# A hybrid decoder block on one Trainium2 core: queries and keys transposed in fp32 and split on the way out of the PSUM bank, key blocks in a ring of three, rotary and softmax steps done for all heads at once

## The chip, the core and the metric

The kernel runs on one core of one Trainium2 chip. The core has five engines with a queue each: TensorE (PE, with its weight loads PEld), VectorE (DVE), ScalarE (ACT), GpSimd (POOL) and SyncE (SP, which here only issues transfers). The metric is the device time of one execution in microseconds (us), and lower is better.

## What is computed

The block takes x of 2048 tokens by 1024 channels through a layer norm, one input projection, windowed attention beside a gated unit, an output projection and a dense feed-forward part. The change lies in the attention:

```python
    q, k, v, su, sv = jnp.split(proj, splits, axis=-1)
    q = apply_partial_rope(q.reshape(b, s, N_Q_HEADS, HEAD_DIM), cos, sin)   # 8 heads of 64, 16 rotated
    k = apply_partial_rope(k.reshape(b, s, N_KV_HEADS, HEAD_DIM), cos, sin)  # 2 heads
    attn = sliding_window_attention(q, k, v, attn_sinks[l])
    ...
    # in sliding_window_attention, blocks of 128 tokens:
    kb, vb = band(k), band(v)                       # the block before and the current one
    scores = jnp.einsum('bnqkgd,bnskd->bnkgqs', qb, kb) * (HEAD_DIM ** -0.5)
    scores = jnp.where(allowed, scores, -1e30)      # each query sees 128 keys
    probs = jax.nn.softmax(jnp.concatenate([scores, sink], axis=-1), axis=-1)[..., :-1]
    out = jnp.einsum('bnkgqs,bnskd->bnqkgd', probs, vb)
```

All products that must be exact to fp32 are made from two reduced-precision parts of each operand, a high part (a rounded copy) and a low part (the value less its high part). "Split" means the making of the two.

## The kernel before

The tokens go through the first stage in 16 tiles of 128. For tile i the functions are, in words: `x_transpose` turns the normalised tile and splits it into `hT` (8 transposes into bank `pst`, an ACT copy for the high part, a DVE subtraction, L159, for the low part); `inproj` makes the key/value projection `pkv` (24 matmuls of 256 columns) and the query projection `pq` (24 of 512); `kv_post` and `q_post` add the bias, rotate 16 of every 64 channels (`rope`), and split the result in SBUF into `ks` and `qs` (L340/341 and L359/360); `k_transpose` turns the four 128-column pieces of `ks`, copies them to `kT` (L370), and copies the block once more (L373) into the next tile's `kT`, so that each tile has its own pair of blocks; `q_transpose` turns the eight pieces of `qs` (L380) and copies them out (L382); `scores` makes 16 matmuls in two groups of four heads (banks `ps_0`, `ps_1`), selects the 128 keys that are seen (`copy_predicated`), takes the maximum, and runs eight exponentials per tile on ACT; `softmax` divides on POOL (L425); `p_transpose` turns the probabilities (`pt`), splits them (`hl`) and masks them on POOL (L443); `pv` multiplies them by v (`po`), and the result is stored.

The main loop (L642) runs tile i's scores beside the projections of tile i+2 and the transposes of tile i+3. POOL's order in this stage is the order of the program (`manual_schedule`). On the other engines a scheduler sets the order when the program is built; each engine then works through its own list strictly in order. The buffers limit it: `ps2` has 2 PSUM buffers of 1024 columns, which `pst`, `ps_0`, `ps_1` and the query transposes take in turn, and `ps1` has 4 of 512 columns, taken in turn by the rest. `ps_1` of a tile lands in the buffer from which `hT` was read just before. POOL does, per tile, two products of the softmax, `x*g_in` (L680), four masks (L443), `x+b_in` (L692) and a small power.

After the 16 tiles come the gated unit (matmuls `psv`, `pu`, `pm`), the output projection (`pw`) and the feed-forward part, which takes from about 710 us to the end. They are not touched.

## Time and profile before

| | |
|---|---|
| median of 3 runs (lowest, highest) | 2070.11 us (2068.48, 2766.5) |
| the profiled execution's own time | 2070.19 us |
| its span, first to last instruction | 2068.5 us |
| mean granted TensorE clock | 0.981 |
| busy: PE, DVE, ACT, POOL | 95%, 70%, 37%, 21% of the span |
| PE, DVE, POOL busy between 100 and 300 us (200 us) | 181.0, 179.5, 133.2 us |
| PE busy between 1000 and 1500 us (500 us) | 499.8 us |

Busy times are sums over an engine's instructions. Over the whole span PE is the bound. In the first 350 us, where the change lies, DVE is as busy as PE. [...]

### The profile page before, as it was taken

Reading aid. Unit: us, or ns where it says so; the run is one execution under the profiler, and the core shown is the slowest. Engines: PE = TensorE matmul, PEld = TensorE weight load, DVE = VectorE, ACT = ScalarE, POOL = GpSimd, SP = SyncE. Lnnn points to the kernel's source line nnn. Section 1 sums busy time; section 2 is a strip of 40 time slices with the busy share of each in tenths; the row PEclk is TensorE's granted clock in tenths of the full one; section 3 lists DMA queues with packets and bytes.
Section 4 is the critical chain, followed back from the end, with each engine's and each line's share of the span. In section 5 each row is a group of like instructions: output and inputs, shape, how many; then the busy total and the mean of one; then the engine's idle time right before and its main releaser. Section 6 shows DMA issues by size and latency. Waiting matters only on the chain.

```text
span 2068.5 us, 25063 instructions
## 1 busy us (share of the span) xinstructions
PE 1967.7 (95%) x9326; PEld 1621.9 (78%) x9326; DVE 1453.0 (70%) x2497; ACT 762.1 (37%) x1484; POOL 443.2 (21%) x378
## 2 busy tenths in 40 slices
...
GB/s 197 97 107 102 108 138 178 239 102 102 182 199 199 105 171 69 84 90 65 90 82 71 120 135 72 92 79 74 92 57 96 229 208 219 188 165 190 160 117 102
DMA packets 137010, 267.60 MB, mean 129 GB/s; under 512 B 8244, under 2 KB 79924, under 8 KB 133304
## 3 DMA queue, kind: packets, MB, share of 16 engines
...
q8 instruction: 73, 1.20, 0.2%
...
## 4 chain that ended last, share of the span: by engine, by line
issue 38%; PE 37%; DVE 14%; DMA 6%; ACT 2%; POOL 2%; SPq 0%; POOLq 0%; ACTq 0%; DVEq 0%
PE X_d L943 10%; PE Z_d L943 5%; PE pu L575 4%; PE psv L537 4%; PE X_g L943 3%; PE Y_d L943 3%; DMA acc<-in_x 2%; DMA h2d<-acc 2%; PE pq L314 2%; PE Z_g L943 1%; PE pw L809 1%; PE pkv L314 1%; POOL aD L993 1%; DVE st L124 1%; DVE acc L798 1%
## 5 line engine op out<-in xcount | busy, mean ns | idle before, releaser
L844 ACT ACTIVATE ws<-s 128x512 fp32r<-128x512 f32 x176 | 109.9, 627 | 303.4 <-PE Z_g L943 152.7
L993 POOL DMA_DIRECT2D aD<-x x44 | 23.5, 534 | 858.4 <-DVE x L991 839.0
L809 PE MATMUL pw<-wo,m 128*128 128x512 f32 x768 | 178.3, 391 | 0.0
L809 PEld LDWEIGHTS pw<-wo,m 128*128 128x128 f32 x768 | 143.0, 188 | 29.1
L845 DVE TENSOR_TENSOR ws<-s,ws 128x512 fp32r<-128x512 f32 x176 | 121.1, 690 | 58.5 <-ACT ws L844 57.1
L943 PE MATMUL Z_g<-t1t_h,ws 128*128 128x512 f32 x528 | 138.0, 398 | 0.5 <-DVE ws L845 0.5
L943 PE MATMUL Y_g<-b21t_h,wa 128*128 128x512 f32 x528 | 137.2, 394 | 0.0
L943 PE MATMUL X_g<-t2t_h,ws 128*128 128x512 f32 x528 | 130.9, 396 | 3.0 <-ACT x L973 3.0
L943 PE MATMUL X_g<-b11t_h,wa 128*128 128x512 f32 x528 | 132.6, 398 | 0.3 <-ACT wa L844 0.3
L943 PE MATMUL Z_g<-b22t_h,ws 128*128 128x512 f32 x528 | 130.4, 395 | 1.7 <-ACT ws L844 1.7
L943 PE MATMUL X_g<-t3t_h,ws 128*128 128x512 f32 x528 | 130.5, 395 | 0.2 <-ACT x L973 0.2
L943 PE MATMUL X_g<-t4t_h,wa 128*128 128x512 f32 x528 | 130.1, 395 | 0.0
L844 ACT ACTIVATE ws_d<-s_d 128x512 fp32r<-128x512 f32 (+1 forms) x96 | 55.7, 593 | 188.8 <-PE X_d L943 51.1
L845 DVE TENSOR_TENSOR wa<-rw,wa 128x512 fp32r<-128x512 f32 x132 | 90.2, 686 | 47.7 <-ACT wa L844 47.5
L943 PEld LDWEIGHTS X_g<-t2t_h,ws 128*128 128x128 f32 x528 | 99.6, 189 | 27.1 <-ACT x L973 3.4
L943 PEld LDWEIGHTS Z_g<-t1t_h,ws 128*128 128x128 f32 x528 | 100.0, 190 | 25.0 <-DVE ws L845 1.0
L943 PEld LDWEIGHTS X_g<-b11t_h,wa 128*128 128x128 f32 x528 | 100.3, 190 | 24.4 <-ACT wa L844 0.7
L943 PEld LDWEIGHTS Z_g<-b22t_h,ws 128*128 128x128 f32 x528 | 99.3, 188 | 25.7 <-ACT ws L844 2.2
L943 PEld LDWEIGHTS X_g<-t3t_h,ws 128*128 128x128 f32 x528 | 99.2, 188 | 24.2 <-ACT x L973 0.7
L943 PEld LDWEIGHTS Y_g<-b21t_h,wa 128*128 128x128 f32 x528 | 99.2, 188 | 23.8 <-ACT wa L844 0.2
L943 PEld LDWEIGHTS X_g<-t4t_h,wa 128*128 128x128 f32 x528 | 99.3, 188 | 23.5
L991 DVE TENSOR_TENSOR x<-X_g,x 128x512 f32<-128x512 f32 x44 | 30.4, 690 | 115.7 <-PE X_g L943 115.7
...
## 6 DMA issues: line engine op xcount, KB each, us to landing
...
hTg<-hTd POOLq DMA_DIRECT2D x16, 1024.0 KB, 10.4
...
```

The lines of the kernel that those rows point to most:

```text
L124: V.bn_stats(st[:, j, :], src[:, j * 512:(j + 1) * 512])
L314: PE.matmul(ps[:, :c1_ - c0], t[:, a, k, :], wq[k][:, b, c0:c1_], start=(k == 0 and n == 0), stop=(k == KT - 1 and n == 2))
L537: PE.matmul(pv_, t[:, a, k, :], wsv_t[k][:, b, :], start=(k == 0 and n == 0), stop=(k == KT - 1 and n == 2))
L575: PE.matmul(pu[:, j, :], wsu_t[k][:, a, hs], t[:, b, k, :], start=(k == 0 and n == 0), stop=(k == KT - 1 and n == 2))
L798: V.tensor_tensor(ac, ac, ag, ALU.mult)
L809: PE.matmul(po[:, c * 512:(c + 1) * 512], m[k // 4][:, a, kc], wo[k][c][:, b, :], start=(k == 0 and n == 0), stop=(k == KT - 1 and n == 2))
L844: A.activation(hi, src, AF.Copy)
L845: V.tensor_tensor(lo, src, f32b(hi), ALU.subtract)
L943: PE.matmul(bank[x_], lt[:, a, k, :], rt[:, b, k, :], start=(first and k == 0 and m == 0), stop=(k == nk - 1 and m == 2), skip_group_check ...
L991: V.tensor_tensor(v["x1"], ps, v["x1"], ALU.mult)
L993: PL.dma_start(aD[g][h][:, e, :], v["o"].rearrange("p a t -> p (a t)"))
```

## The change

- **Queries and keys.** They are no longer split in SBUF. `kv_post` writes each key head twice and the values into one fp32 tile `qkv` (tag `qs`, now two buffers), `q_post` adds the queries. PE turns that tile: two transposes for the keys instead of four, four for the queries instead of eight. The split happens out of PSUM: ACT copies the high part, DVE subtracts for the low part (L355 and L369 of the new file). For queries this is done in two halves of 64 partitions.
- **Key ring.** `kT` is one tile with three blocks; the copy of a block for the next tile goes.
- **Rotary.** One pass of three DVE instructions over 12 heads (8 query heads and 4 key copies) takes the place of two passes of four.
- **Scale.** The factor 1/8 moves from the query's bias step into the exponential.
- **Softmax.** The shift `nm`, the sink term `es`, the sum and the reciprocal are made once for 8 heads instead of twice for 4; both groups' maxima come first, and then all eight exponentials.
- **Banks.** The query transposes take a `ps1` buffer and no longer a `ps2` buffer. Loads and tiles that borrowed the old tags borrow other ones.

```diff
     def qbias():
         V.tensor_scalar(nsink, sink, -1.0, None, ALU.mult)
 
-        V.tensor_scalar(bqkv[:, :ATTN], bqkv[:, :ATTN], SCALE, None, ALU.mult)
...
-    kTt = {}
+
+    kT = c1.tile([P, NKV, 2, 3, P], F32R, name="kT")
     vd = {}
     qTt = {}
-
-    def new_kT(i):
-        kTt[i] = wk.tile([P, NKV, 2, 2, P], F32R, tag="kT", name=f"kT{i}")
-
-    new_kT(0)
...
-    def rope(i, t, nh, nm):
-        rot = t.rearrange("p (h d) -> p h d", d=HD)[:, :, :ROT]
-        rot = rot.rearrange("p h (a b) -> p h a b", a=2)
-        t1 = wk.tile([P, nh, 2, HALF], F32, tag="rt1" + nm, bufs=1, name=f"rt1{nm}_{i}")
-        t2 = wk.tile([P, nh, 2, HALF], F32, tag="rt2" + nm, bufs=1, name=f"rt2{nm}_{i}")
-        cb = cos2[:, i].unsqueeze(1).broadcast_to([P, nh, 2, HALF])
-        V.tensor_tensor(t1, rot, cb, ALU.mult)
-        for a in range(2):
-            sb = sin2[:, i, a].unsqueeze(1).broadcast_to([P, nh, HALF])
-            V.tensor_tensor(t2[:, :, a], rot[:, :, 1 - a], sb, ALU.mult)
-        V.tensor_tensor(rot, t1, t2, ALU.add)
+
+    NR = NQ + 2 * NKV
 
     def kv_post(i):
         ps = pproj.pop((i, "kv"))
-        kv = wk.tile([P, QKV - ATTN], F32, tag="kv", bufs=1, name=f"kv{i}")
-        V.tensor_tensor(kv, ps[:, :QKV - ATTN], bqkv[:, ATTN:], ALU.add)
-        rope(i, kv[:, :P], NKV, "k")
-        ks = wk.tile([P, NKV, 2, 2, HD], F32R, tag="ks", bufs=1, name=f"ks{i}")
-        kb = kv[:, :P].rearrange("p (g d) -> p g d", g=NKV).unsqueeze(2)
-        kb = kb.broadcast_to([P, NKV, 2, HD])
-        A.activation(ks[:, :, 0], kb, AF.Copy)
-        V.tensor_tensor(ks[:, :, 1], kb, f32b(ks[:, :, 0]), ALU.subtract)
-        qks[i, "k"] = ks
-        qks[i, "v"] = kv
+        t = wk.tile([P, NR * HD + P], F32, tag="qs", name=f"qkv{i}")
+        kk = [v_.rearrange("p (g d) -> p g d", g=NKV).unsqueeze(2).broadcast_to([P, NKV, 2, HD])
+              for v_ in (ps[:, :P], bqkv[:, ATTN:ATTN + P])]
+        V.tensor_tensor(t[:, ATTN:NR * HD].rearrange("p (g e d) -> p g e d", g=NKV, e=2), *kk,
+                        ALU.add)
+        V.tensor_tensor(t[:, NR * HD:], ps[:, P:2 * P], bqkv[:, ATTN + P:], ALU.add)
+        qks[i] = t
 
     def v_post(i):
-        kv = qks.pop((i, "v"))
-        v3 = kv[:, P:].rearrange("p (g d) -> p g d", g=NKV)
+        v3 = qks[i][:, NR * HD:].rearrange("p (g d) -> p g d", g=NKV)
         vd[i] = wk.tile([P, NKV, 2, HD], F32R, tag="vd", bufs=4, name=f"vd{i}")
         A.activation(vd[i][:, :, 0], v3, AF.Copy)
         V.tensor_tensor(vd[i][:, :, 1], v3, f32b(vd[i][:, :, 0]), ALU.subtract)
 
     def q_post(i):
         ps = pproj.pop((i, "q"))
-        q = wk.tile([P, ATTN], F32, tag="q", bufs=1, name=f"q{i}")
-        V.scalar_tensor_tensor(q, ps, SCALE, bqkv[:, :ATTN], ALU.mult, ALU.add)
-        rope(i, q, NQ, "q")
-        q3 = q.rearrange("p (h d) -> p h d", d=HD)
-        qs = wk.tile([P, NQ, 2, HD], F32R, tag="qs", bufs=1, name=f"qs{i}")
-        V.tensor_copy(qs[:, :, 0, :], q3)
-        V.tensor_tensor(qs[:, :, 1, :], q3, f32b(qs[:, :, 0, :]), ALU.subtract)
-        qks[i, "q"] = qs
+        t = qks[i]
+        V.tensor_tensor(t[:, :ATTN], ps, bqkv[:, :ATTN], ALU.add)
+        rot = t[:, :NR * HD].rearrange("p (h d) -> p h d", d=HD)[:, :, :ROT]
+        rot = rot.rearrange("p h (a b) -> p h a b", a=2)
+        t1 = wk.tile([P, NR, 2, HALF], F32, tag="rt1q", bufs=1, name=f"rt1_{i}")
+        t2 = wk.tile([P, NR, 2, HALF], F32, tag="rt2q", bufs=1, name=f"rt2_{i}")
+        cb = cos2[:, i].unsqueeze(1).broadcast_to([P, NR, 2, HALF])
+        sb = sin2[:, i].unsqueeze(1).broadcast_to([P, NR, 2, HALF])
+        V.tensor_tensor(t1, rot, cb, ALU.mult)
+        V.tensor_tensor(t2, rot[:, :, ::-1, :], sb, ALU.mult)
+        V.tensor_tensor(rot, t1, t2, ALU.add)
 
     def k_transpose(i):
-        ks = qks.pop((i, "k"))
-        pk = ps1.tile([P, 512], F32, tag="one", name=f"pk{i}")
-        kf = f32b(ks.rearrange("p g a b d -> p (g a b d)"))
-        for j in range(4):
-            PE.transpose(pk[:, j * P:(j + 1) * P], kf[:, j * P:(j + 1) * P], ident)
-        pk4 = pk.rearrange("p (g a t) -> p g a t", g=NKV, a=2)
-        A.activation(kTt[i][:, :, :, 1, :], pk4, AF.Copy)
-        if i + 1 < NT:
-            new_kT(i + 1)
-            V.tensor_copy(kTt[i + 1][:, :, :, 0, :], f32b(kTt[i][:, :, :, 1, :]))
+        pk = ps1.tile([P, 512], F32, tag="one", name=f"pk{i}")[:, :NKV * P]
+        for g in range(NKV):
+            c = (NQ + 2 * g) * HD
+            PE.transpose(pk[:, g * P:(g + 1) * P], qks[i][:, c:c + P], ident)
+        pk = pk.rearrange("p (g t) -> p g t", g=NKV)
+        r = i % 3
+        A.activation(kT[:, :, 0, r, :], pk, AF.Copy)
+        V.tensor_tensor(kT[:, :, 1, r, :], pk, f32b(kT[:, :, 0, r, :]), ALU.subtract)
 
     def q_transpose(i):
-        qs = qks.pop((i, "q"))
-        pq = ps2.tile([P, D], F32, tag="two", name=f"pq{i}")
-        qf = f32b(qs.rearrange("p h a d -> p (h a d)"))
-        for j in range(NQ):
-            PE.transpose(pq[:, j * P:(j + 1) * P], qf[:, j * P:(j + 1) * P], ident)
-        qT = wk.tile([P, NQ, P], F32R, tag="qT", bufs=1, name=f"qT{i}")
-        A.activation(qT.rearrange("p h t -> p (h t)"), pq, AF.Copy)
+
+
+        pq = ps1.tile([P, 512], F32, tag="one", name=f"pq{i}")
+        for j in range(NQ // 2):
+            PE.transpose(pq[:, j * P:(j + 1) * P], qks[i][:, j * P:(j + 1) * P], ident)
+        qks.pop(i)
+        qT = wk.tile([P, 2, NQ // 2, P], F32R, tag="qT", bufs=1, name=f"qT{i}")
+        for e in range(2):
+            own, other = slice(e * HD, (e + 1) * HD), slice((1 - e) * HD, (2 - e) * HD)
+            hi = qT[own, e].rearrange("p h t -> p (h t)")
+            A.activation(hi, pq[own], AF.Copy)
+            V.tensor_tensor(qT[other, e].rearrange("p h t -> p (h t)"), pq[own], f32b(hi),
+                            ALU.subtract)
         qTt[i] = qT
 
     pr = {}
 
     def scores(i):
         qT = qTt.pop(i)
-        kT = kTt.pop(i)
-        c0 = 1 if i == 0 else 0
+        r = i % 3
+        blocks = slice(r, r + 1) if i == 0 else (slice(0, 3, 2) if r == 0 else slice(r - 1, r + 1))
+        cur = 1 if r or i == 0 else 0
         mx = wk.tile([P, NQ], F32, tag="mx", name=f"mx{i}")
         nm = wk.tile([P, NQ], F32, tag="nm", name=f"nm{i}")
         sm = wk.tile([P, NQ], F32, tag="sm", name=f"sm{i}")
         es = wk.tile([P, NQ], F32, tag="es", name=f"es{i}")
+        pbs = []
         for g in range(NKV):
-            ps = ps2.tile([P, G, 2 * P], F32, tag="two", name=f"ps{i}_{g}")
+            ps = ps2.tile([P, G, 2, P], F32, tag="two", name=f"ps{i}_{g}")
             pb = wk.tile([P, G, P], F32, tag="pb", bufs=3, name=f"pb{i}_{g}")
             for j in range(G):
                 for a in range(2):
-                    PE.matmul(ps[:, j, c0 * P:], qT[:, g * G + j, :],
-                              kT[:, g, a, c0:].rearrange("p c t -> p (c t)"),
-                              start=(a == 0), stop=(a == 1))
+                    PE.matmul(ps[:, j, 1:] if i == 0 else ps[:, j], qT[:, j % 2, (g * G + j) // 2, :],
+                              kT[:, g, a, blocks], start=(a == 0), stop=(a == 1))
             if i == 0:
                 PL.memset(pb, NEG)
             else:
-                A.activation(pb, ps[:, :, :P], AF.Copy)
-            V.copy_predicated(pb, curb, ps[:, :, P:])
+                A.activation(pb, ps[:, :, 1 - cur], AF.Copy)
+            V.copy_predicated(pb, curb, ps[:, :, cur])
             gs = slice(g * G, (g + 1) * G)
             V.tensor_reduce(mx[:, gs], pb, op=ALU.max, axis=mybir.AxisListType.X)
-            V.scalar_tensor_tensor(nm[:, gs], mx[:, gs], -1.0, nsink[:, gs], ALU.mult, ALU.min)
-            V.tensor_tensor(es[:, gs], sink[:, gs], nm[:, gs], ALU.add)
-            for j in range(G):
-                h = g * G + j
-                A.activation(pb[:, j, :], pb[:, j, :], AF.Exp, bias=nm[:, h:h + 1],
-                             accum_out=sm[:, h:h + 1])
-            A.activation(es[:, gs], es[:, gs], AF.Exp)
-            pr[i, g] = (pb, sm, es)
+            pbs.append(pb)
+        V.scalar_tensor_tensor(nm, mx, -SCALE, nsink, ALU.mult, ALU.min)
+        V.tensor_tensor(es, sink, nm, ALU.add)
+        for h in range(NQ):
+            pb = pbs[h // G][:, h % G, :]
+            A.activation(pb, pb, AF.Exp, bias=nm[:, h:h + 1], scale=SCALE,
+                         accum_out=sm[:, h:h + 1])
+        A.activation(es, es, AF.Exp)
+        pr[i] = (pbs, sm, es)
 
     def softmax(i):
-        for g in range(NKV):
-            pb, sm, es = pr[i, g]
+        pbs, sm, es = pr[i]
+        V.tensor_tensor(sm, sm, es, ALU.add)
+        V.reciprocal(sm, sm)
+        for g, pb in enumerate(pbs):
             gs = slice(g * G, (g + 1) * G)
-            V.tensor_tensor(sm[:, gs], sm[:, gs], es[:, gs], ALU.add)
-            V.reciprocal(sm[:, gs], sm[:, gs])
             PL.tensor_tensor(pb, pb, sm[:, gs].unsqueeze(2).broadcast_to([P, G, P]), ALU.mult)
 
...
-            tag, bufs = (("rq", 2), ("rq", 2), ("kT", 2), ("qs", 1))[j]
+            tag, bufs = (("rq", 2), ("rq", 2), ("qs", 2), ("qs", 2))[j]
...
-            gv = wk.tile([P, SGW], F32, tag="ks" if e else "q", bufs=1, name=f"gv{i}")
+            gv = wk.tile([P, SGW], F32, tag="qT" if e else "gv", bufs=1, name=f"gv{i}")
```

What the scheduler does with it on two engines, in the tile whose scores are number 9 (of 0 to 15). First TensorE, before: the piece from the transposes of tile 12 (`pst`) over the scores of tile 9 (`ps_0`, `ps_1`), the turning of tile 8's probabilities (`pt`) and tile 7's products with v (`po`) to the first matmuls of the next key projection (`pkv`).

```order
L156 MATMUL pst_2452<-ident,x_1870 128x128 x8
L400 MATMUL ps_0_2531<-kT_2174,qT_2396 128x256 x7
L434 MATMUL pt_0_2466<-ident,pb_0_2315 128x128 x4
L400 MATMUL ps_0_2531<-kT_2174,qT_2396 128x256
L434 MATMUL pt_1_2477<-ident,pb_1_2335 128x128 x4
L461 MATMUL po_0_2489<-pT_0_2263,vd_1650 128x512 x2
L461 MATMUL po_0_2489<-pT_0_2263,vd_1867 128x512 x2
L461 MATMUL po_1_2497<-pT_1_2274,vd_1650 128x512 x2
L461 MATMUL po_1_2497<-pT_1_2274,vd_1867 128x512 x2
L400 MATMUL ps_1_2551<-kT_2174,qT_2396 128x256 x8
L314 MATMUL pkv_2571<-wq_237,hT_2451 128x256 x3
```

`pst` stands right behind the query projection and ahead of the scores, and `ps_1`, which lands in the buffer of `pst`, comes 2 us of PE work later. The same piece of the changed kernel:

```order
L390 MATMUL ps_0_2302<-kT,qT_2179 128x256 x2
L390 MATMUL ps_1_2315<-kT,qT_2179 128x256 x2
L390 MATMUL ps_0_2302<-kT,qT_2179 128x256 x6
L390 MATMUL ps_1_2315<-kT,qT_2179 128x256 x6
L423 MATMUL pt_0_2237<-ident,pb_0_2108 128x128 x4
L423 MATMUL pt_1_2248<-ident,pb_1_2121 128x128 x4
L450 MATMUL po_0_2260<-pT_0_2056,vd_1509 128x512 x2
L450 MATMUL po_0_2260<-pT_0_2056,vd_1704 128x512 x2
L450 MATMUL po_1_2268<-pT_1_2067,vd_1509 128x512 x2
L450 MATMUL po_1_2268<-pT_1_2067,vd_1704 128x512 x2
L156 MATMUL pst_2418<-ident,x_1902 128x128 x8
L308 MATMUL pkv_2339<-wq_237,hT_2222 128x256 x3
```

`pst` has moved behind the scores and `po`: `ps_1` no longer follows it, and a whole tile of work lies between `pst` and the next use of its buffer. Over all tiles 0 to 13 the last `pst` transposes stand between the query projection and the scores in 13 before and in 5 now. Both groups' scores now stand together, the first two of each group ahead of the other six. The four query transposes stand behind `pkv` and the key transposes, ahead of the next query projection.

Then VectorE for the same tile, before, from the first selection (`pb_0`) to the first shift (`nm`) of tile 9:

```order
L407 COPY_PREDICATED pb_0_2532<-curm,ps_0_2531 128x512
L124 BN_STATS st<-x_2726 128x6 x2
L437 TENSOR_TENSOR hl_1_2482<-pt_1_2477,hl_1_2482 128x512
L466 TENSOR_TENSOR at_2488<-po_0_2489,plo_0_2494 64x512
L350 TENSOR_TENSOR vd_2506<-kv_2398,vd_2506 128x2x64
L466 TENSOR_TENSOR at_2488<-po_1_2497,plo_1_2502 64x512
L409 TENSOR_REDUCE mx_2527<-pb_0_2532 128x4
L407 COPY_PREDICATED pb_1_2552<-curm,ps_1_2551 128x512
L125 BN_AGGR mv<-st 128x2
L335 TENSOR_TENSOR kv_2615<-pkv_2571,bqkv 128x256
L410 SCALAR_TENSOR_TENSOR nm_2528<-mx_2527,nsink 128x4
```

and now:

```order
L396 COPY_PREDICATED pb_0_2303<-curm,ps_0_2302 128x512
L398 TENSOR_REDUCE mx_2298<-pb_0_2303 128x4
L426 TENSOR_TENSOR hl_0_2242<-pt_0_2237,hl_0_2242 128x512
L396 COPY_PREDICATED pb_1_2316<-curm,ps_1_2315 128x512
L426 TENSOR_TENSOR hl_1_2253<-pt_1_2248,hl_1_2253 128x512
L455 TENSOR_TENSOR at_2259<-po_0_2260,plo_0_2265 64x512
L331 TENSOR_TENSOR vd_2277<-qkv_2184,vd_2277 128x2x64
L398 TENSOR_REDUCE mx_2298<-pb_1_2316 128x4
L455 TENSOR_TENSOR at_2259<-po_1_2268,plo_1_2273 64x512
L159 TENSOR_TENSOR hT_2417<-pst_2418,hT_2417 128x1024
L400 SCALAR_TENSOR_TENSOR nm_2299<-mx_2298,nsink 128x8
```

The first shift stood behind one maximum; the second stood five rows further. Now the one shift stands behind both maxima and behind the subtraction for `hT`, and all eight exponentials wait for it. Behind it, in the same list, the sum `sm` waits for the exponentials, and the second half of the query split and the query's bias step stand behind `sm`.

## Rows read from the trace of the kernel before

**Rows 1.** Eleven tile periods: stretch, length, busy of PE, PEld, DVE, ACT, POOL, clock, DMA.

```profile
191.10:213.27 22.17, 16.80 (x97) 14.53 (x95) 20.33 (x43) 12.44 (x37) 15.91 (x13) 0.92 0.32 120
213.27:228.64 15.37, 15.37 (x103) 13.85 (x102) 13.03 (x31) 9.22 (x26) 10.13 (x9) 1.00 0.27 102
...
sum 195.87, PE 176.88 PEld 154.71 DVE 177.36 ACT 118.81 POOL 132.12; mean PE 16.08 PEld 14.06 DVE 16.12 ACT 10.80 POOL 12.01
```

**Rows 2.** Groups by line, PE, 99.85 to 295.72: busy, mean ns, idle before.

```profile
L400 PE MATMUL ps<-kT,qT 128*128 128x256 f32 x176 | 28.9, 306 | 12.1 <-DVE hT L159 10.4 <-ACT qT L382 1.7
...
L434 PE MATMUL pt<-ident,pb 128*128 128x128 f32 x88 | 13.7, 284 | 5.4 <-POOL pb L425 5.4
```

**Rows 3.** Timeline of PE: start, length, what, idle before and its releaser.

```profile
206.56 1.22 PE L400 MATMUL ps<-kT,qT 128*128 128x256 f32 x8 [3.82 <-DVE hT L159]
```

**Rows 4.** Timeline of DVE ahead of that wait.

```profile
201.42 2.76 DVE L360 TENSOR_TENSOR qs<-q,qs 128x512 fp32r<-128x512 f32 x1
...
205.30 1.20 DVE L159 TENSOR_TENSOR hT<-pst,hT 128x1024 fp32r<-128x1024 f32 x1
```

**Rows 5.** Timeline of POOL, the same and the next tile.

```profile
201.08 2.55 POOL L680 TENSOR_TENSOR x<-x,g_in 128x1024 f32<-128x1024 f32 x1 [0.90 <-ACT x L139]
...
217.43 1.08 POOL L425 TENSOR_TENSOR pb<-pb,sm 128x512 f32<-128x512 f32 x1 [0.37 <-DVE sm L424]
```

**Rows 6.** Groups by line, DVE, 99.85 to 295.72.

```profile
L360 DVE TENSOR_TENSOR qs<-q,qs 128x512 fp32r<-128x512 f32 x11 | 16.7, 1519 | 0.1
...
L410 DVE SCALAR_TENSOR_TENSOR nm<-mx,nsink 128x4 f32<-128x4 f32 x21 | 11.3, 538 | 0.0
L411 DVE TENSOR_TENSOR es<-sink,nm 128x4 f32<-128x4 f32 x22 | 10.7, 486 | 0.0
...
L329 DVE TENSOR_TENSOR rt2q<-q,sin 128x64 f32<-128x64 f32 x22 | 8.3, 413 | 0.0
L326 DVE TENSOR_TENSOR rt1q<-q,cos 128x128 f32<-128x128 f32 x11 | 8.1, 736 | 0.3
...
L373 DVE CAST kT<-kT 128x512 fp32r<-128x512 f32 x11 | 7.0, 639 | 0.5 <-ACT kT L370 0.5
...
L326 DVE TENSOR_TENSOR rt1k<-kv,cos 128x32 f32<-128x32 f32 x11 | 5.3, 485 | 0.0
L359 DVE CAST qs<-q 128x512 fp32r<-128x512 f32 x11 | 5.3, 485 | 0.4
...
L329 DVE TENSOR_TENSOR rt2k<-kv,sin 128x16 f32<-128x16 f32 x22 | 4.2, 217 | 0.0
...
L330 DVE TENSOR_TENSOR q<-rt1q,rt2q 128x128 f32<-128x128 f32 x11 | 3.2, 291 | 0.3
```

**Rows 7.** Timeline of PE in an unbroken tile period.

```profile
220.67 0.60 PE L434 MATMUL pt<-ident,pb 128*128 128x128 f32 x4
...
224.46 3.12 PE L314 MATMUL pkv<-wq,hT 128*128 128x256 f32 x24
227.41 1.04 PE L380 MATMUL pq<-ident,qs 128*128 128x128 f32 x8
228.28 0.60 PE L368 MATMUL pk<-ident,ks 128*128 128x128 f32 x4
228.64 0.71 PE L314 MATMUL pq<-wq,hT 128*128 128x512 f32 x2
```

**Rows 8.** Two DVE subtractions by line: count, shortest/median/longest ns.

```profile
L360 DVE TENSOR_TENSOR qs<-q,qs x16: 676/684/2758, 47.6 to 312.3; 128x512 fp32r<-128x512 f32 x16
...
L437 DVE TENSOR_TENSOR hl<-pt,hl x32: 625/674/691, 76.7 to 341.1; 128x512 fp32r<-128x512 f32 x32
```

**Rows 9.** Timelines at the start: PE, then DVE.

```profile
55.93 0.90 PE L368 MATMUL pk<-ident,ks 128*128 128x128 f32 x3 [2.58 <-DVE ks L341]
...
19.38 1.75 DVE L288 TENSOR_SCALAR bqkv<-bqkv 128x512 f32<-128x512 f32 x1
```

**Rows 10.** The last weight loads (`rsu`) into borrowed buffers, from issue to landing.

```profile
DMA to landing us min/median/max: 4.9/4.9/4.9
```

5 lines of the change are left out of this document (2 added, 3 removed).

## The prediction

> **What bounds the kernel now.** I looked first at the busy shares by slices of time: after 710 us TensorE is busy nearly without a break, and the change touches nothing there. The loop that it touches was then cut into tile periods, each from the start of one tile's query projection to the start of the next. Eleven of them fill 195.87 us, so a tile takes 17.81 us. TensorE is busy for 16.08 us of it and VectorE for 16.12 [rows 1]: neither is the bound by itself, and each loses time to the other. One period shows what TensorE needs when nothing holds it: 15.37 us, all 103 matmuls recorded, no idle time, clock 1.00. [...] So a mean tile loses 17.81 - 15.37 = 2.44 us: 195.87 - 176.88 = 18.99 us of waiting over eleven tiles, 1.73 each, and 16.08 - 15.37 = 0.71 of matmuls that run slower, mostly in periods that had waits.
>
> The groups by line say whom TensorE waits for: the scores for VectorE's subtraction that makes `hT`, 10.4 us in eleven tiles (0.95 a tile), and the turning of the probabilities for POOL's product, 5.4 us (0.49) [rows 2]. One case in the timelines: at 206.56 the scores start after a wait of 3.82 us for `hT` [rows 3]. VectorE made that `hT` at 205.30, late because its subtraction for the query split (L360) took 2.76 us [rows 4]. The usual length of that one is 0.684 [rows 8]. Beside it POOL ran `x*g_in` from 201.08 for 2.55 us, to 203.63 [rows 5], and the subtraction ended at 204.18, just behind. I read this as VectorE held while POOL works on SBUF. L437, a subtraction of the same shape that reads a PSUM bank, is 625 to 691 ns in all 32 cases; L360, which reads SBUF alone, goes from 676 to 2758 [rows 8].
>
> **The change, part by part.** The profiled execution took 2070.19 us, the median is 2070.11, so the sum may be set against either. Tiles 0 to 13 go through this loop, fourteen periods.
>
> *TensorE.* Eight query transposes take 228.28 - 227.41 = 0.87 us of its queue, 0.109 each, and four key transposes 0.36, 0.09 each [rows 7]. Four and two fall away: 0.435 + 0.18 = 0.62 us a tile. The unbroken period goes from 15.37 to 14.75. Score and projection matmuls keep shape and number; the ring's strided blocks and the other bank I cost at nothing, as weights and columns are as many as before.
>
> *VectorE* [rows 6]. The rotary of the queries is 0.736 + 2 x 0.413 + 0.291 = 1.85 us, of the keys 0.485 + 2 x 0.217 = 0.92 without its small add. Three passes over 192 elements replace them: at least the element-wise share at the speed of the add, 3 x 0.291 x 1.5 = 1.31, at most one at the speed of L326 and two halves more of L329's, 0.736 x 1.5 + 0.826 x 1.5 = 2.34 with the add inside; I take 1.8, in the middle, and save 1.0. The copy of the key block (0.639) goes. Cast and subtraction of the query split (0.485 + 1.519 = 2.00) become two subtractions out of PSUM on half the partitions; I take L437's 0.674 for each, since the columns are as many, and save 0.65. One `nm` and one `es` fewer: 0.538 + 0.486 = 1.02. The values' separate bias step is new, about the 0.291 of the query's rotary add. The key split's subtraction keeps its size. Saved: 1.0 + 0.64 + 0.65 + 1.02 - 0.29 = 3.0 us, so VectorE falls from 16.1 to about 13.1 us a tile, below TensorE's 14.75. TensorE becomes the bound.
>
> [...]
>
> *The wait for `hT`, 0.95 a tile.* `ps_1` waits for it because it lands in the buffer that `pst` held a moment before. The order rows show `pst` behind the query projection and right ahead of the scores in 13 tiles before and in 5 now. In the others a whole projection lies between, which covers it. And the L360 that was late is gone: its successor reads PSUM. I leave 5/14 of 0.95, about 0.3. Bounds: 0 (all covered) and 0.95.
>
> *The wait for the probabilities.* Here the change costs. Formerly each group had its own shift and exponentials; now all eight wait for one `nm` behind both maxima. The chain today, from the end of `ps_1` (206.56 + 1.22 = 207.78 [rows 3]) to the end of POOL's second product (217.43 + 1.08 = 218.51 [rows 5]), is 10.7 us. Now a product of the first group, 1.08, stands in it as well: 11.8; and where `hT` stands ahead of `nm`, as in the order rows, 1.20 more [rows 4]: 13.0. A POOL block of one of its SBUF steps adds at most 2.758 - 0.684 = 2.07 [rows 8]. What covers it is TensorE's work until `pt`. Where `pt` stands behind all scores of the next tile that is a full period, 14.75, and nothing waits. In about half of the tiles `pt` and `po` come behind only two of the scores: the stretch from `pt` to `pkv`, 224.46 - 220.67 = 3.8 us, and six more score matmuls of 256 columns, 0.74 at the 0.123 of `pkv`'s 24 (227.41 - 224.46 = 2.95), no longer cover: 14.75 - 3.8 - 0.74 = 10.2 [rows 7]. There TensorE waits some 11.8 - 10.2 = 1.6 us. Seven tiles of 1.6 and seven of 0.3 (an occasional block) give 0.95 a tile; bounds 0 (a chain of 10.2 or less) and 2.8 (13.0 in every tile, under the short cover). Behind `sm`, which waits for the exponentials, VectorE's list holds the second query-split half and the query's bias step; those are late next, with the next tile's scores behind them.
>
> *Sum of the loop.* 14.75 + 0.3 + 0.95 = 16.0 us a tile. Of the 0.71 us of slower matmuls I keep nothing, since it sits in periods with long waits, such as the one at clock 0.92; were all of it to stay, it would cost 14 x 0.71 = 10 us. 17.81 - 16.0 = 1.81, times 14 is 25 us.
>
> *Start.* The scaling of the bias row (1.75 us on VectorE at 19.38) goes, and so does TensorE's 2.58 us wait for the first key split (at 55.93) [rows 9], in whose place the bank's split follows the transposes and other matmuls fill. Both may be hidden behind the loads: bounds 0 and 4.3, and I take 3.
>
> *End of the loop and later.* The last weight loads take other borrowed buffers and land 4.9 us after issue [rows 10], with the gated unit's first matmuls ahead of their use; without that cover they cost up to 4.9. The factor in the exponential costs nothing, ACT being idle a third of the tile (10.80 of 17.81 busy) [rows 1]. All later stages shift unchanged.
>
> Result: 2070 - 25 - 3 = **2042 us**. With the two waits together between half and one and a half of their 1.25 (9 us either way) or the slower matmuls kept, the likeliest case alone runs from 2033 to 2052.
>
> **Rivals.**
>
> *A, no waits.* The chain fits its cover and `hT` is never late: 14.75 a tile, 17.81 - 14.75 = 3.06, times 14 is 43, and 3 at the start: **2024**. For it: VectorE's load falls by 3 us a tile and the SBUF-only steps that POOL can hold are far fewer. Against it: 11.8 us do not fit in 10.2, and the first wait of the chain is for eight exponentials in a row.
>
> *B, the waits only change their name.* The scores wait for `qT`'s second half or the probabilities for `sm`, as long as today: only the transposes are saved, 14 x 0.62 = 9: **2061**. For it: an `nm` or `sm` at the head of VectorE's strict list holds the query split behind it. Against: VectorE then has 3 us less to catch up with.
>
> [...]
>
> *D, no change in effect.* The order between the engines gives back the gain but no more, 2066 to 2074; I count it with B's upper side.
>
> **How the numbers follow.** My forecast (2033 to 2052) 0.61, A 0.16, B with D 0.18, C 0.05. A change within 2% (41 us, about what a measurement of this kernel can tell from none) ends at 2029. Faster by more: A, less the part of it that has small waits, 0.14, and a sliver of the forecast's lower edge, 0.01: 0.15. Slower by more, 2111: of C its greater half, 0.03. Within: 0.82. For 8 in 10 I leave out C, B's part above 2060 with D, and A's lowest: 2024 to 2060.
>
> **What would show it.** Right: tile periods near 16 us; VectorE's busy time per tile near 13; the scores' idle time for `hT` down to a third; the two query-split subtractions as steady as L437; `pt` waiting for `pb` in about half the tiles. Wrong: scores waiting for `qT` over 1 us a tile (B); several periods with a clock near 0.92 or a chain over 13.3 us from the scores to the second product (C); no `pt` wait at all (A); or a later stage that isn't as long as now.

## The result and the profile after

The changed kernel takes 2055.19 us (median of 4 runs, 2054.23 to 2056.66) against 2071.43 us before in the same session: a ratio of 0.9927, with a 95% interval of 0.9907 to 0.9946. One of the four runs before was a slow one of 2766.5 us; the median of the other three is 2070.11 us, so that the change saves some 15 us, where 28 were forecast: inside the range (2024 to 2060), outside the likeliest case's own one (2033 to 2052), and within 2%.

Two rows divide the program where the attention part ends. They give the matmuls of the output projection (`pw`), with the shortest, median and longest time in ns and the starts of the first and the last. Before:

```profile
L809 PE MATMUL pw<-wo,m x768: 387/389/481, 520.5 to 717.4; 128*128 128x512 f32 x192
```

And after:

```profile
L798 PE MATMUL pw<-wo,m x768: 387/389/628, 509.2 to 705.7; 128*128 128x512 f32 x192
```

`pw` starts at 520.5 before and 509.2 after, so 11.3 us are gained ahead of it. From there to the end of the span it takes 2068.5 - 520.5 = 1548.0 and 2052.7 - 509.2 = 1543.5 us. The code of that part is the same, so 11.3 of the 15.8 us between the two spans lie where the change is; the other 4.5 come from a part that it does not touch. Over the kernels below this part takes 1541.3 to 1552.8 us, each in one profiled execution. Medians that lie a few us apart say little about the attention for this reason, and the table below shows both numbers.

The 11.3 us divide at the starts of the query projections (the first matmul) of tile 3 and tile 15. Twelve periods lie between, in windows of time (stretch, length, busy of PE, PEld, DVE, ACT, POOL with their instructions, granted TensorE clock as a share of full speed, DMA share, GB/s). Before:

```profile
79.83:295.72 215.89, 194.46 (x1198) 170.09 (x1197) 193.18 (x431) 131.49 (x362) 144.74 (x111) 0.97 0.28 105
```

After:

```profile
78.31:284.16 205.85, 185.51 (x1120) 159.86 (x1118) 177.38 (x316) 126.79 (x349) 139.02 (x111) 0.98 0.29 109
```

Up to tile 3 the kernel is 79.83 - 78.31 = 1.5 us ahead. The twelve periods take 205.85 instead of 215.89 us, 17.15 instead of 17.99 a tile, which is 10.0 us. From tile 15 to `pw` it is 225.0 against 224.8. So the start gave half of what was forecast (3), and the loop too: 0.84 us a tile where 1.81 was forecast (16.0 from 17.81). Much hangs on one tile: the period of tile 3, which the eleven periods of [rows 1] leave out, fell from 20.0 to 16.1 us. Over those eleven a tile takes 17.81 before and (284.16 - 94.42) / 11 = 17.25 now, 0.56 less.

Of the 17.15 us TensorE is busy for 15.46 (before 194.46 / 12 = 16.20) and idle for 1.70 (before 1.79). The idle time has other names now. Groups by line, PE, the twelve periods of the changed kernel (busy, mean ns, idle before and who ended it):

```profile
L308 PE MATMUL pkv<-wq,hT 128*128 128x256 f32 x288 | 36.6, 282 | 1.7 <-DVE hl L426 1.7
L390 PE MATMUL ps<-kT,qT 128*128 128x256 f32 x192 | 28.9, 290 | 10.0 <-DVE qT L369 6.9 <-DVE hT L159 3.0
...
L423 PE MATMUL pt<-ident,pb 128*128 128x128 f32 x96 | 14.7, 290 | 4.2 <-POOL pb L415 4.0
L156 PE MATMUL pst<-ident,x 128*128 128x128 f32 x89 | 12.1, 276 | 2.9 <-DVE pb L396 2.8
```

The scores' wait for `hT` is 3.0 us in twelve tiles, where [rows 2] had 10.4 in eleven. In its place they wait 6.9 for `qT`. The wait for POOL's product is 4.0. A wait of `pst` for VectorE is new (2.8), and that of `pkv` has grown (1.7, before 0.9).

VectorE is busy for 177.38 / 12 = 14.78 us a tile (before 193.18 / 12 = 16.10), not 13.1. Its groups by line and shape, the same stretch:

```profile
L369 DVE TENSOR_TENSOR qT<-pq,qT 64x512 fp32r<-64x512 f32 x24 | 16.5, 689 | 4.7 <-ACT qT L368 4.0
...
L343 DVE TENSOR_TENSOR rt<-qkv,cos 128x192 f32<-128x192 f32 x12 | 15.7, 1308 | 0.4
...
L400 DVE SCALAR_TENSOR_TENSOR nm<-mx,nsink 128x8 f32<-128x8 f32 x13 | 10.4, 799 | 0.1
...
L344 DVE TENSOR_TENSOR rt<-qkv,sin 128x192 f32<-128x192 f32 x12 | 8.6, 713 | 0.0
...
L401 DVE TENSOR_TENSOR es<-sink,nm 128x8 f32<-128x8 f32 x12 | 8.2, 682 | 0.1
```

L369, the query split out of PSUM, takes its 689 ns as expected. The steps with both operands in SBUF are longer than their like in [rows 6]: the rotary product with `cos` 1308 ns for 192 elements (736 for 128 there), `nm` 799 (538), `es` 682 (486).

One tile shows how this becomes a wait. Timelines of POOL, DVE, ACT and PE in that order (start, length, what, idle before and its releaser):

```profile
111.43 2.40 POOL L681 TENSOR_TENSOR x<-x,b_in 128x1024 f32<-128x1024 f32 x1
...
119.76 2.40 POOL L669 TENSOR_TENSOR x<-x,g_in 128x1024 f32<-128x1024 f32 x1
...
112.98 0.88 DVE L400 SCALAR_TENSOR_TENSOR nm<-mx,nsink 128x8 f32<-128x8 f32 x1
...
117.69 0.68 DVE L369 TENSOR_TENSOR qT<-pq,qT 64x512 fp32r<-64x512 f32 x1
...
119.44 0.69 DVE L369 TENSOR_TENSOR qT<-pq,qT 64x512 fp32r<-64x512 f32 x1 [0.34 <-ACT qT L368]
120.17 2.20 DVE L343 TENSOR_TENSOR rt<-qkv,cos 128x192 f32<-128x192 f32 x1
...
123.06 1.22 DVE L159 TENSOR_TENSOR hT<-pst,hT 128x1024 fp32r<-128x1024 f32 x1
...
113.89 0.40 ACT L404 ACTIVATE pb<-pb,nm 128x128 f32<-128x128 f32 x1 [3.02 <-DVE nm L400]
...
117.09 0.57 ACT L368 ACTIVATE qT<-pq 64x512 fp32r<-64x512 f32 x1
...
118.43 0.50 PE L390 MATMUL ps<-kT,qT 128*128 128x256 f32 x2 [1.06 <-DVE qT L369]
...
124.34 1.22 PE L390 MATMUL ps<-kT,qT 128*128 128x256 f32 x8 [1.27 <-DVE hT L159]
```

POOL's `x+b_in` runs from 111.43 to 113.83. VectorE's `nm`, issued into it at 112.98, ends at 113.86, and ACT's first exponential starts at 113.89. Eight of them take until 117, and the copy of the query's high part stands behind them in ACT's list, at 117.09, although PE had made its transposes by 110.9. So the subtraction is at 117.69, and the scores start at 118.43 after 1.06 us of waiting. Then `x*g_in` runs from 119.76 to 122.16, the rotary product issued at 120.17 takes 2.20 us, `hT`'s subtraction behind it comes at 123.06, and the second group's scores wait 1.27 us for it. Two steps of POOL stand behind two waits of TensorE. Of the first wait the hold explains at most 0.7 us: `nm` took 0.88, and its median in e2 below is 0.17.

### The profile page after: what moved, and what is told of

It is laid out like the page before. It is cut to its first block, busy times and chain, and to the rows that moved or that the text cites. A ratio compares the mean times of both kernels' runs of the same rounds, so it can differ in the third digit from the quotient of the medians.

```text
span 2052.7 us, 24699 instructions
## 1 busy us (share of the span) xinstructions
PE 1956.4 (95%) x9230; PEld 1611.6 (79%) x9230; DVE 1431.7 (70%) x2353; ACT 754.0 (37%) x1468; POOL 442.6 (22%) x378
## 4 chain that ended last, share of the span: by engine, by line
PE 65%; DVE 11%; issue 7%; DMA 4%; ACT 2%; POOL 2%; SPq 0%; POOLq 0%; DVEq 0%; ACTq 0%
PE X_g L932 21%; PE Z_g L932 11%; PE X_d L932 8%; PE Y_g L932 5%; PE Z_d L932 4%; PE pu L564 4%; PE pw L798 3%; PE psv L526 3%; PE Y_d L932 2%; DMA acc<-in_x 1%; DMA h2d<-acc 1%; ACT pb L404 1%; DVE da L1022 1%; DVE b_d L897 1%; PE pm L577 1%
## 6 DMA issues: line engine op xcount, KB each, us to landing
hTg<-hTd POOLq DMA_DIRECT2D x16, 1024.0 KB, 10.2
```

## The experiments

Two theories were set against each other. **H**: VectorE's steps between SBUF operands are held while POOL runs its long steps; the hold moves to whichever step comes next, and so the loop got less than the sum said. **S**: the single softmax chain for eight heads costs what was to be gained.

With each edit the scheduler sets the order of PE, DVE and ACT anew, so a few us between two kernels can be the order's. All results, with the mean tile period over twelve tiles, the start of `pw` and the time from there to the end, each from the kernel's profile:

| kernel | median us | ratio to before (95%) | tile us | `pw` starts | rest |
|---|---|---|---|---|---|
| before | 2069.9 to 2072.2 | 1 | 17.99 | 520.5 | 1548.0 |
| changed | 2055.2 | 0.9907 to 0.9946 | 17.15 | 509.2 | 1543.5 |
| e1 softmax by group | 2053.1 | 0.9883 to 0.9917 | 16.74 | 502.6 | 1549.5 |
| e2 no affine, changed | 2040.1 | 0.9830 to 0.9859 | 15.46 | 486.4 | 1551.7 |
| e3 no affine, before | 2041.6 | 0.9838 to 0.9868 | 15.99 | 494.1 | 1546.7 |
| e4 x*g_in earlier | 2058.1 | 0.9917 to 0.9947 | 17.35 | 509.3 | 1550.8 |
| e5 quarters | 2045.8 | 0.9859 to 0.9897 | 16.39 | 498.2 | 1541.3 |
| e6 rotary in two passes | 2055.9 | 0.9913 to 0.9945 | 17.30 | 511.0 | 1545.9 |
| e8 split, ring and bank only | 2053.9 | 0.9904 to 0.9933 | 17.14 | 502.9 | 1547.7 |
| e10 quarters and by group | 2049.3 | 0.9870 to 0.9904 | 16.05 | 497.4 | 1546.3 |
| e11 affine on VectorE | 2061.8 | 0.9943 to 0.9975 | 17.16 | 510.6 | 1548.8 |
| e13 bank back | 2061.9 | 0.9935 to 0.9965 | 17.43 | 510.7 | 1550.4 |
| e14 transposes twice | 2051.6 | 0.9885 to 0.9920 | 17.10 | 507.9 | 1543.4 |
| e15 sum on POOL | 2078.5 | 1.0028 to 1.0050 | 17.96 | 522.4 | 1552.8 |

### POOL's two steps left out (e2, e3)

```diff
         if i + 5 < NT:
             x_normalize(xt[i + 5], i + 5)
-            PL.tensor_tensor(xt[i + 5], xt[i + 5], g_in, ALU.mult)
...
-            PL.tensor_tensor(xt[i + 5], xt[i + 5], b_in, ALU.add)
```

> The changed kernel with GpSimd's two steps x*g_in and x+b_in left out for tiles 5 to 15 (the scale and shift of the layer norm are missing there). Theory H: the rotary product falls from 1.31 us in the mean to under 0.45, nm and es from 0.80 and 0.68 to about 0.2, VectorE's busy time from 14.4 to about 12 us a tile, and the period from 17.1 to 15.5 to 16, eleven tiles: 2037 to 2043 us. Theory S: the chain of exponentials stays, the period falls by no more than 0.5 us: 2049 to 2055 us.

> The kernel before with the same two steps of GpSimd left out for tiles 5 to 15. Theory H, strict form (the hold hides the change's gain): the pair without the hold shows the gain that the forecast had, some 25 to 30 us between this and the changed kernel without the steps, so 2064 to 2070 us here. Theory H, wide form (before loses as much to the hold as after): 2050 to 2058 us here, with the query split's subtraction at 0.68 us in every tile, and again some 15 us to the changed kernel. Theory S: under 5 us to the changed kernel without the steps.

The changed kernel falls by 15 us to 2040.1, the kernel before by some 30 to 2041.6. The twelve periods of e2 in one window, and two of its VectorE groups (the rotary product and `nm`):

```profile
76.85:262.42 185.57, 177.81 (x1120) 156.16 (x1117) 152.94 (x315) 126.15 (x349) 91.68 (x91) 1.00 0.33 121
...
L343 DVE TENSOR_TENSOR rt<-qkv,cos 128x192 f32<-128x192 f32 x12 | 6.8, 568 | 0.4
L400 DVE SCALAR_TENSOR_TENSOR nm<-mx,nsink 128x8 f32<-128x8 f32 x12 | 5.4, 449 | 0.1
```

The twelve periods of e3:

```profile
77.01:268.84 191.83, 185.67 (x1206) 164.97 (x1205) 162.36 (x433) 129.96 (x362) 95.70 (x91) 1.00 0.32 119
```

And its scores in these periods, with the query split by line (shortest, median, longest ns):

```profile
L400 PE MATMUL ps<-kT,qT 128*128 128x256 f32 x192 | 28.8, 289 | 0.6 <-ACT qT L382 0.6
...
L360 DVE TENSOR_TENSOR qs<-q,qs x16: 674/680/1130, 47.7 to 284.0; 128x512 fp32r<-128x512 f32 x16
```

VectorE does the same work in e2 as in the changed kernel, and is busy for 152.94 / 12 = 12.74 us a tile instead of 14.78. In e3 it is 162.36 / 12 = 13.53 instead of 16.10, and L360 never takes over 1.13 us, where [rows 8] had up to 2.758. So these two steps hold VectorE for 2.04 us a tile now and for 2.57 before, and without them TensorE waits little in either kernel: 14.82 busy of 15.46, and 15.47 of 15.99, at clock 1.00 in both. What POOL's other steps hold is still there: the rotary product and `nm` in e2 (568 and 449 ns) did not fall to the 450 and 200 that were expected. In e3 the scores do not wait for `hT` at all, though the bank is as before; the 10.4 us of [rows 2] came with the hold.

e2's time is the one that H gave. e3's is in none of its three cases: 2041.6 lies under all ranges, and the 1.5 us between the two medians are what S was given (under 5). The wide form is right that the kernel before loses as much to the hold as the changed one (it loses more), and wrong that some 15 us of the change stay without it. The strict form, by which the whole forecast gain appears once the hold is gone, fell. In the twelve periods the change is worth 191.83 - 185.57 = 6.3 us without the two steps, against 10.0 with them; in the eleven from tile 4 on it is 2.1 (172.98 - 170.92) against 6.1. So between a third and some three fifths of the loop's gain stay without the two steps, and the rest is less of the hold.

What VectorE's steps really save can be read here: 13.53 - 12.74 = 0.79 us a tile (0.6 over the eleven periods), not 3.0.

The median times leave 1.5 us between the two kernels, the starts of `pw` 7.7; the part behind `pw` took 5.0 us longer in e2's profile, and why is open.

### x*g_in moved (e4)

```diff
+            if 1 <= i < NT - 4:
+                PL.tensor_tensor(xt[i + 4], xt[i + 4], g_in, ALU.mult)
             softmax(i)
...
-            PL.tensor_tensor(xt[i + 5], xt[i + 5], g_in, ALU.mult)
...
-        if i + 5 < NT:
-            PL.tensor_tensor(xt[i + 5], xt[i + 5], b_in, ALU.add)
+        if 1 <= i < NT - 4:
+            PL.tensor_tensor(xt[i + 4], xt[i + 4], b_in, ALU.add)
```

> The changed kernel with GpSimd's x*g_in moved, nothing left out: each tile's product runs one step of the loop later, ahead of the softmax products instead of behind them, where GpSimd idles some 3.5 us for the sum while VectorE waits for the exponentials too; x+b_in follows as before. Theory H: the rotary product, now held by x*g_in in most tiles (2.2 us instead of 0.35), is free, its mean falls from 1.31 to under 0.7 us and hT's subtraction behind it comes earlier: 2042 to 2050 us. Theory S: 2053 to 2060 us, or later where the product of the softmax now stands behind x*g_in.

2058.1: the expected gain did not come, and the time lies in the range of S. H's mechanism is there, its forecast of the place was wrong. Timelines of POOL, then DVE:

```profile
110.91 2.40 POOL L644 TENSOR_TENSOR x<-x,g_in 128x1024 f32<-128x1024 f32 x1
...
110.90 2.43 DVE L400 SCALAR_TENSOR_TENSOR nm<-mx,nsink 128x8 f32<-128x8 f32 x1
...
115.14 0.36 DVE L343 TENSOR_TENSOR rt<-qkv,cos 128x192 f32<-128x192 f32 x1
```

The rotary product is free now (0.36 us), but `nm` is issued at 110.90 as `x*g_in` starts at 110.91, and takes 2.43 us until that ends. All eight exponentials wait behind `nm`. Moving the step moved the hold to another VectorE step in front of something, here to `nm`; no other place was tried.

### The same steps in quarters (e5), and with the softmax by group (e10)

```diff
-            PL.tensor_tensor(xt[i + 5], xt[i + 5], g_in, ALU.mult)
+            for c in range(4):
+                cs = slice(c * 256, (c + 1) * 256)
+                PL.tensor_tensor(xt[i + 5][:, cs], xt[i + 5][:, cs], g_in[:, cs], ALU.mult)
```

and the same for `b_in`; e10 has the edit of e1 (below) beside it.

> The changed kernel with GpSimd's x*g_in and x+b_in made in four pieces of 256 columns each, nothing left out. If the hold lasts to the end of the GpSimd instruction that runs and VectorE gets its turn between two of them, no VectorE step takes over about 1.1 us (its own 0.35 to 0.45 and a piece of 0.6 to 0.7), against 2.5 now, and the time falls to 2043 to 2050 us. If VectorE gets no turn between pieces that follow each other at once, the longest steps stay at 2.3 us or more and the time at 2053 to 2060 us.

> The changed kernel with GpSimd's two steps in four pieces each and the softmax steps per group of four heads again, nothing left out. If the two effects are apart (shorter holds, shorter softmax chain), some 2 to 5 us under the pieces alone: 2040 to 2044 us. If the pieces leave nothing for the chain to give: 2044 to 2050 us, as the pieces alone.

e5 takes 2045.8 us, in the range of the first case: the best of the kernels that compute everything, 9 us under the changed one. POOL, DVE, and the twelve periods in one window:

```profile
117.30 3.18 POOL L671 TENSOR_TENSOR x<-x,g_in 128x256 f32<-128x256 f32 x4
...
117.73 0.51 DVE L343 TENSOR_TENSOR rt<-qkv,cos 128x192 f32<-128x192 f32 x1
118.17 0.89 DVE L344 TENSOR_TENSOR rt<-qkv,sin 128x192 f32<-128x192 f32 x1
119.09 0.78 DVE L345 TENSOR_TENSOR qkv<-rt,rt 128x192 f32<-128x192 f32 x1
...
78.06:274.71 196.65, 184.50 (x1119) 161.85 (x1118) 163.73 (x316) 126.41 (x350) 150.91 (x173) 0.97 0.31 114
```

VectorE gets its turn between the pieces: the three rotary steps take 0.51, 0.89 and 0.78 us while the four pieces run from 117.30 to 120.48, where one whole step had held the first of them for 2.20. POOL pays for it, its four pieces take 3.18 us instead of 2.40. VectorE is at 163.73 / 12 = 13.64 us a tile, between the 14.78 with whole steps and 12.74 without. The longest `nm` and `es` still take 1.19 and 1.21 us. This run also answers a rival for e2, that POOL merely had less to do there: here POOL is busy for 150.91 us in the twelve periods, more than in the changed kernel (139.02), and the kernel is faster all the same.

e10 took 2049.3, with an interval that overlaps e5's. Its loop is 0.34 us a tile shorter and `pw` starts 0.8 us earlier, while the part behind takes 5.0 us longer. The runs don't tell the two apart.

### The same steps on VectorE (e11)

```diff
-            PL.tensor_tensor(xt[i + 5], xt[i + 5], g_in, ALU.mult)
+            V.tensor_tensor(xt[i + 5], xt[i + 5], g_in, ALU.mult)
```

and the same for `b_in`.

> The changed kernel with x*g_in and x+b_in made on VectorE for tiles 5 to 15 instead of GpSimd, nothing left out: 2.4 us more work for VectorE a tile (1.2 each by hT's subtraction of the same size), but no 2.4 us step beside it. If the hold is what costs: VectorE at 12.7 + 2.4 = 15.1 us a tile, a little over TensorE's 14.8, periods of 15.8 to 16.5: 2045 to 2053 us. If VectorE's own load is what costs: 14.4 + 2.4 = 16.8 us a tile and 2062 to 2075 us.

2061.8 us, just under the second case. The twelve periods in one window, and the two steps' groups:

```profile
80.57:286.48 205.91, 184.41 (x1119) 160.09 (x1117) 176.23 (x338) 126.96 (x351) 97.65 (x91) 0.98 0.29 105
...
L669 DVE TENSOR_TENSOR x<-x,g_in 128x1024 f32<-128x1024 f32 x10 | 13.5, 1354 | 1.1 <-ACT x L139 1.1
L681 DVE TENSOR_TENSOR x<-x,b_in 128x1024 f32<-128x1024 f32 x10 | 12.9, 1285 | 0.1
```

VectorE is busy for 176.23 / 12 = 14.69 us, about the 12.74 without hold and (13.5 + 12.9) / 12 = 2.2 of the new steps. The period is 17.16, as in the changed kernel (17.15). A hold costs here what the same time of VectorE's own work costs. I read this as VectorE staying on the path at 14.7 us a tile, though TensorE's matmuls alone need 14.8: the two take turns. That VectorE falls below TensorE did not make it free.

### Softmax by group, rotary in two passes, and both (e1, e6, e8)

```diff
-        V.scalar_tensor_tensor(nm, mx, -SCALE, nsink, ALU.mult, ALU.min)
-        V.tensor_tensor(es, sink, nm, ALU.add)
-        for h in range(NQ):
+            V.scalar_tensor_tensor(nm[:, gs], mx[:, gs], -SCALE, nsink[:, gs], ALU.mult, ALU.min)
+            V.tensor_tensor(es[:, gs], sink[:, gs], nm[:, gs], ALU.add)
+            for j in range(G):
```

(e1; the sum and the reciprocal are made by group too). e6 takes the rotary apart, with four steps for the keys in `kv_post` and four for the queries in `q_post`:

```diff
+        rope(i, t[:, ATTN:NR * HD], 2 * NKV, "k")
...
+        rope(i, t[:, :ATTN], NQ, "q")
-        V.tensor_tensor(t1, rot, cb, ALU.mult)
-        V.tensor_tensor(t2, rot[:, :, ::-1, :], sb, ALU.mult)
-        V.tensor_tensor(rot, t1, t2, ALU.add)
```

and e8 has both edits.

> The changed kernel with one part undone: shift, sink term, sum and reciprocal are made per group of four heads again, each group's exponentials right behind its own maximum. Theory H (VectorE's steps between SBUF operands are held while GpSimd runs x*g_in and x+b_in, and this hold ate the loop's gain): no gain, since four more small SBUF steps a tile can be held: 2055 to 2063 us. Theory S (the single softmax chain for eight heads ate it): the 9 us of the forecast's waits come back, 2043 to 2048 us, and TensorE's idle time before pt (9.0 us in all tiles) and before ps for qT (7.6 us) falls to half.

> The changed kernel with the rotary undone: keys (four copies) and queries apart, four VectorE steps each. By the prediction's sum (1.0 us a tile, from means that contain the hold, with VectorE on the path) 2063 to 2070 us. By the theory that the hold belongs to GpSimd's steps and only moves to whichever VectorE step comes next, the rotary's own time matters: 1.72 us unheld in two passes against 1.06 in one, VectorE being below TensorE's busy time: 2053 to 2060 us.

> The changed kernel with both the rotary and the softmax steps as before: what stays is the split out of the PSUM bank, the ring and the bank change. If these carry the gain (fewer transposes, and the 128x512 split step no longer exposed to the hold): 2050 to 2060 us. If the merged steps carry it: 2064 to 2072 us.

e6: 2055.9, no difference from 2055.2, as H has it; the rotary in one pass is worth nothing that these runs show. e8: 2053.9, so the split, the ring and the bank bring the whole gain, and the merged steps none that the totals show. No run takes the split and the ring apart.

e1 lies between the two expectations. Its median is 2 us under the changed kernel, with overlapping intervals; in its profile `pw` starts 6.6 us earlier, the part behind takes 6.0 us longer. Its PE groups over the twelve tiles:

```profile
L390 PE MATMUL ps<-kT,qT 128*128 128x256 f32 x192 | 30.6, 303 | 10.4 <-DVE qT L369 7.5 <-DVE hT L159 2.7
...
L423 PE MATMUL pt<-ident,pb 128*128 128x128 f32 x96 | 14.6, 288 | 2.6 <-POOL pb L415 2.6
```

The wait for the probabilities falls from 4.0 to 2.6, as S says, the one for `qT` does not (7.5, from 6.9). e8's `pw` start (502.9) is near e1's (502.6), 8.1 us ahead of e6's. So both profiles say that merging the softmax costs 6 to 8 us in the attention, but not in the same place: e1 has 5 us of it in the twelve periods, e8 against e6 only 1.9. The totals say 2 us. S may have the sign right; its size is open.

### The bank back (e13)

```diff
-        pq = ps1.tile([P, 512], F32, tag="one", name=f"pq{i}")
+        pq = ps2.tile([P, D], F32, tag="two", name=f"pq{i}")[:, :512]
```

> The changed kernel with one part undone: the query transposes take a buffer of the two-buffer pool again, in turn with pst and the scores. If the bank change and the order that follows from it took the scores' wait for hT away (10.4 us in eleven tiles before, 3.0 in twelve now), the wait returns and the time is 2060 to 2068 us. If another wait ends last anyway: 2053 to 2059 us.

2061.9 us falls in the first case's range, but not by its mechanism. PE groups over the same twelve tiles:

```profile
L390 PE MATMUL ps<-kT,qT 128*128 128x256 f32 x192 | 28.2, 291 | 6.3 <-DVE hT L159 4.0 <-DVE qT L369 2.1
...
L423 PE MATMUL pt<-ident,pb 128*128 128x128 f32 x96 | 17.1, 312 | 16.3 <-POOL pb L415 16.3
```

`hT`'s wait is 4.0, hardly more than 3.0, though `pst` stands ahead of the scores in all twelve tiles. The one for the probabilities is four times as long; the order puts all of `pt` and `po` ahead of the scores in eight of the twelve. The tile period is 17.43 against 17.15, 3.3 us in twelve, yet `pw` starts only 1.5 us later; 6.9 us are lost behind `pw`. So the bank's own worth in the loop is small if any, and the loss behind is not explained.

### The transposes made twice (e14)

```diff
-        for j in range(NQ // 2):
+        for j in list(range(NQ // 2)) * 2:
             PE.transpose(pq[:, j * P:(j + 1) * P], qks[i][:, j * P:(j + 1) * P], ident)
```

and the same for the two key transposes.

> The changed kernel with its four query and two key transposes made twice, which gives TensorE the transposes of before again without any other change. By the prediction's term of 0.62 us a tile for fourteen tiles TensorE's work is on the path throughout: +8.7 us, 2062 to 2066 us. If TensorE's waits for other engines absorb it: 2054 to 2059 us.

2051.6 us, under both ranges and not slower at all. The twelve periods:

```profile
77.13:282.30 205.17, 188.60 (x1191) 164.62 (x1190) 176.12 (x317) 125.86 (x349) 142.51 (x112) 0.99 0.28 105
```

TensorE is busy for 188.60 / 12 = 15.72 us instead of 15.46, and its idle time falls from 1.70 to 1.38. The six transposes are taken up in part by its waits. In part they come back elsewhere: busy time rose by 0.26 and not by 0.62, with a mean granted clock of 0.99 where the changed kernel has 0.98. I read from this that taking them out lowers the period only where TensorE has no wait; of the changed kernel's twelve periods that is one (253.94 to 269.40, busy for 15.46 of 15.46 us).

### The sum on POOL (e15)

```diff
-        V.tensor_tensor(sm, sm, es, ALU.add)
-        V.reciprocal(sm, sm)
+        PL.tensor_tensor(sm, sm, es, ALU.add)
+        PL.tensor_tensor(sm, sm, mone, ALU.pow)
```

> The changed kernel with the softmax's sum and reciprocal made on GpSimd (an add and a power of -1, two small steps of about 0.55 us each by its power step) instead of VectorE, nothing left out. If VectorE's sum, waiting for the exponentials ahead of the query split's second half, is what makes the scores wait for qT (7.6 us in all tiles): that wait falls under 2 us and the time to 2044 to 2050 us. If the softmax chain, now 0.7 us longer through GpSimd, ends last: TensorE's wait for the probabilities grows from 9 to 15 us or more and the time is 2054 to 2062 us.

2078.5 us, and neither case. The groups of PE, DVE and POOL in the twelve periods:

```profile
L392 PE MATMUL ps<-kT,qT 128*128 128x256 f32 x192 | 29.0, 300 | 9.8 <-DVE qT L371 9.7
...
L425 PE MATMUL pt<-ident,pb 128*128 128x128 f32 x96 | 14.6, 290 | 0.7 <-POOL pb L417 0.6
L158 PE MATMUL pst<-ident,x 128*128 128x128 f32 x88 | 12.7, 291 | 12.9 <-DVE pb L398 12.8
...
L371 DVE TENSOR_TENSOR qT<-pq,qT 64x512 fp32r<-64x512 f32 x24 | 16.5, 689 | 11.5 <-ACT qT L370 11.1
...
L414 POOL TENSOR_TENSOR sm<-sm,mone 128x8 f32<-128x8 f32 x12 | 19.8, 1652 | 0.9
```

The scores' wait for `qT` grows from 6.9 to 9.7: VectorE's L371 itself waits 11.1 us for ACT's copy (4.0 in the changed kernel). It was not VectorE's sum that held the split, it is ACT's list, where the query copies stand behind the eight exponentials, as the tile at 117.09 above showed. The wait for the probabilities is all but gone (0.6), so the softmax chain does not end last either. The power step takes 1.65 us for 8 columns, not 0.55, and `pst` now waits 12.8 us for the selection (`pb`) on VectorE. How much of the 23 us each of these costs was not taken apart.

## Why the prediction was right in its range and wrong in its sum

**TensorE's own work: size right, worth wrong.** The unbroken period of e2, 14.82 busy at clock 1.00, answers to the forecast 14.75 [rows 7]. But e14 puts the transposes back and loses nothing. A tile's sum of 14.75 + waits treats the waits as fixed beside the work; in e14 they shrank when TensorE got more to do.

**VectorE, the step that failed.** "Saved: 3.0 us, so VectorE falls to about 13.1" came out as 16.10 - 14.78 = 1.3 us. The durations were means of [rows 6], and these held POOL's time inside. Without the hold (medians by line in e3 and e2) the query split goes from 0.427 + 0.680 to 2 x 0.690, which costs 0.27 where 0.65 was to be saved; `nm` and `es` give 0.29 and not 1.02; the sum and the reciprocal, which the prediction left out, give 0.31. By the medians of all changed lines it is 1.1 us; the busy times above, with what POOL's other steps hold, show 0.6 to 0.8. The rest of the subtracted time was hold, and it did not go with the instructions that showed it. It fell on the rotary product (1308 ns), `nm` and `es` instead. The mechanism stood in the prediction ("VectorE held while POOL works on SBUF"), and the range 625 to 691 against 676 to 2758 was read right; the sum then used the held means as if they were work.

**The subtractions out of PSUM.** Each was priced at L437's 674 ns [rows 8], with nothing added for the new place, and that was near: L369 out of PSUM has a median of 688 ns (690 in e2), L360 out of SBUF 680 without the hold (e3), 8 to 10 ns apart.

**The wait for `hT`: right in size.** 0.25 us a tile (3.0 / 12), 0.3 forecast. Of the two reasons given the second is borne out: e3 has no such wait with L360 unheld and the bank as before, and e13 with the bank back has hardly more (4.0).

**The wait for the probabilities: less than forecast.** 4.0 / 12 = 0.33 against 0.95. Earlier waits in the tile, for `qT` and `hT`, may have given the longer chain cover, but that is not shown: e2, where the scores wait 0.8 us in all, has 4.5 here.

**The new waits: left out of the sum.** Scores for `qT` 6.9 / 12 = 0.58, `pst` 0.24, `pkv` 0.14. Rival B named the first of them ("the scores wait for `qT`'s second half"); the sum had no term for it. It also looked for the cause in the wrong list, VectorE's `sm`; it stands in ACT's (e15). All idle time together is 1.70 us against 1.25 forecast.

**The slower matmuls: wrong.** "Of the 0.71 us of slower matmuls I keep nothing" rested on waits becoming short. TensorE is busy for 15.46, 0.71 over 14.75 (0.64 over e2's 14.82): all of it stayed, the bound of 10 us. With 0.45 more of waiting, 16.0 + 0.71 + 0.45 is the 17.15 of the profile to a hundredth.

**Start: 1.5 where 3 was forecast, and not by its mechanism.** TensorE's wait of 2.58 us for the first key split was to be filled. In its place it waits longer, for the first rotary:

```profile
51.24 0.66 PE L351 MATMUL pk<-ident,qkv 128*128 128x128 f32 x2 [4.42 <-DVE qkv L345]
```

**Rivals.** The loop's gain, 0.84 us a tile over twelve periods and 0.56 over eleven, is near B's 0.62: the waits changed their names. But B's 0.62 were the transposes, and by e14 these are not what was gained, so that its number came near is luck. A's condition, no waits, was not met even in e2. C, the 0.05 for a slower kernel, did not occur: the periods at a clock near 0.9 are three of twelve (0.90 to 0.91), where the kernel before had four (0.91 to 0.92), and no run shows that waits alone bring the clock down. The 13.3 us of chain in its sign, the short cover of 10.2 and A's 3.06 together, is an estimate.

**The last 4.5 us** lie behind `pw`, in equal code, and no step of the prediction had them. Without them the changed kernel would stand near 2060, at the edge of the range and close to B's 2061. That the time lies well inside the range is in part luck.
